# Moving the value splits and half of two normalisations between an attention loop and its output projection

## The chip, the cores and the metric

The kernel runs on one core of one Trainium2 chip. The metric is the device time of one execution in microseconds (us). The engines are TensorE (PE in the profile, its weight loads PEld), VectorE (DVE), ScalarE (ACT), GpSimd (POOL) and SyncE (SP), which issues most DMAs here.

## What is computed

The reference is a trunk of two layers over 1024 tokens of width 1024, in float32. In each layer three groups of attention heads work side by side on one input projection: A (4 heads, a 2-D neighbourhood), B (6 heads, a sliding window with a sink) and C (6 heads, dense). Each group's output is normalised over its own width, the three are joined, and one output projection follows. A gated feed-forward part closes the layer.

```python
ya = neighborhood_attention(...)          # width 256
yb = sliding_window_attention(...)        # width 384
yc = axial_attention(...)                 # width 384
ga, gb, gc = split_cols(g_group[l], GROUP_WIDTHS)
y = jnp.concatenate([rms_norm(ya, ga), rms_norm(yb, gb), rms_norm(yc, gc)], axis=-1)
x = x + gt_a * (y @ w_o[l])
```

## The kernel before

The kernel is written with a framework that traces the program, then orders each engine's instructions by its own estimate of their times. An instruction may be drawn ahead of others that stand before it in the text, unless it is pinned: `pin(engines, True)` makes each instruction of these engines follow the one that was pinned before it. All instructions pass through one helper, so the profile shows them under line 49.

Accuracy comes from splitting: a float32 operand is written as a high part `hi` in a matmul type and a low part `lo` with the rest, and a product takes three matmuls (`mm3`). ScalarE makes `hi`, VectorE makes `lo` from it.

The attention is a loop of steps n from -4 to 66 over a stream of 64 pairs (a pair is one head with 256 queries): pairs 0 to 23 are the C heads, 24 to 39 the A heads, 40 to 63 the B heads; A and B are the "band" heads. In a band step n:

- pair n + 4 is scored (TensorE, `sA` or `sB`, and VectorE adds the bias and takes the row's extreme value), pair n + 3 goes through the exponential (ScalarE), pair n + 2 is divided by its sums (a reciprocal on VectorE, `pr<-pr,rs` on GpSimd);
- pair n is transposed (`T<-identr,pr`) and split (`pt`: ScalarE the high part, VectorE the low part, the latter in step n + 1);
- pair n - 2 is multiplied with the values (`pv`); after every second pair ScalarE copies half of the result (`cmb`), in an odd step, and VectorE combines it into `y` at the start of the next step (`y<-pv,cmb`). One PSUM buffer holds `pv`, so the next pair's product waits for the combine.

In these steps TensorE, ScalarE, VectorE and GpSimd are pinned. After each step's body the list `later` runs what was noted for it, and a few things at fixed steps, unpinned but for GpSimd.

`y` holds the joined output as 8 chunks of 128 channels by 1024 tokens: chunks 0 and 1 are A, 2 to 4 B, 5 to 7 C. The output projection takes the chunks in the order `korder = (5, 6, 7, 0, 1, 2, 3, 4)` and works first on the first 512 tokens ("half 0"), then on the second ("half 1").

When a group's heads are done, its squares are summed in `gss` (tiles `gsq` on the way). `stats` then sums over channels with 16 one-column matmuls (`ps_st`) and takes the reciprocal root by Newton steps on VectorE (`isq`, `rstd`). `norm_scale` turns the roots into a row for each half (`spread`: four transposes into `ps_r`; ScalarE copies it to `rb`, of which there are two buffers shared with `gsq`) and returns one multiply per chunk and half (`y<-y,rb`). For C the statistics come at step 29, both spreads at step 32 and the six multiplies at steps 33 to 38; for A they come at 47, 50 and 51 to 54; all ten multiplies are on GpSimd. B's follow in the output projection, half on VectorE and half on GpSimd.

`y_split(k, half, hi, lo)` scales a chunk by its gain and splits it: one ScalarE and one VectorE instruction. For half 0 of chunks 5, 6, 7, 0, 1 the result lies in `yq` (`qk<-y` in the profile). Two of these five calls stand at steps 55 and 59, three in the output projection after its first weight block (`ki == 0`). Half 0 of the B chunks goes to `yb`, half 1 of all chunks to `y1` later (`y<-y,vecs` in the profile).

In the tail of the loop (from step 60) matmuls of the output projection for the first two chunks (`o_rows(0, ...)`, `o_rows(1, ...)`, into `ps_o`) stand between the last pairs, and weights of the projection are split (`whi`, `wlo`).

Of the kernel before, what the change touches and what calls it, by code (L numbers as in the profile page):

```python
# [85 lines left out]
def trunk(ctx: ExitStack, tc, A, C, out):  # L86
# [320 lines left out]
    def rstd_cols(ssqs, width, nt, sp_, psp, tag="mm", newton=False):  # L407

        ps = psp.tile([P, 512], F32, name="ps_st", tag=tag)
        for j in range(nt):  # L410
            for i, s in enumerate(ssqs):
                pe.matmul(
                    ps[:, j : j + 1],
                    s[:, j * P : (j + 1) * P],
                    ones,
                    start=(i == 0),
                    stop=(i == len(ssqs) - 1),
                )
        r = sp_.tile([P, 8], F32, name="rstd", tag="rstd", bufs=2)
        if newton:  # L420
            inv_sqrt(r[:, :nt], ps[:, :nt], width, sp_)
            return r
        act.activation(r[:, :nt], ps[:, :nt], AF.Sqrt, bias=epst, scale=1.0 / width)
        dve.reciprocal(r[:, :nt], r[:, :nt])
        return r
# [441 lines left out]
    for l in range(2):  # L867
# [770 lines left out]
            square(sq)  # L1638
            pool.tensor_tensor(out=ss[:, c], in0=ss[:, c], in1=sq, op=ALU.add)

        def norm_scale(chunks, r, psp, tag, engines):

            todo = []
            for half, eng in enumerate(engines):
                c = slice(half * H, (half + 1) * H)
                ps = spread(r, 4 * half, psp, tag=tag)
                rb = atp.tile([P, H], F32, name="rb", tag="rb", bufs=2)
                act.copy(rb, ps)
                for n in chunks:
                    todo.append(  # L1650
                        lambda eng=eng, n=n, c=c, rb=rb: eng.tensor_tensor(
                            out=y[:, n, c], in0=y[:, n, c], in1=rb, op=ALU.mult
                        )
                    )
            return todo
# [58 lines left out]
            23: ((5, 6, 7), 384.0), 39: ((0, 1), 256.0), 63: ((2, 3, 4), 384.0),  # L1714
        }
        begins = {23: 0, 39: 24, 63: 40}
        later = {}
        N = len(stream)
        pairs = {}
# [4 lines left out]
        for n in range(-AHEAD - 1, N + 3):  # L1724
            ahead = AHEAD if n + AHEAD < NC else AHEAD_B
            begin = range(done, min(n + ahead + 1, N))
            if n < 0:
                begin = range(done, done)
            elif n == 0:
                opened(*(pairs[i] for i in range(4)))  # L1730
                begin = range(3, 4)
                fresh = []
            elif n < NC:
                for i in range(2 if n > 1 else 0):
                    if 0 <= n:
                        pairs[n].turn(i)
                    while unfinished:
                        unfinished.pop(0)()
                    if 2 <= n - 1:
                        pairs[n - 1].pv(i)  # L1740
                    for m in begin:
                        if m < min(made, NC):
                            pairs[m].qk(i)
                for i in range(2 if n == 1 else 0):
                    pairs[begin[0]].qk(i)
                fresh = [pairs[m] for m in begin if NC <= m < made]
                for b in fresh:
                    b.scores()
                    b.exps()
                    b.divide()  # L1750
            else:
                for b in worked:
                    b.divide()
                if NC <= n - 1 < N:
                    pairs[n - 1].low()
                if NC <= n - 3:
                    pairs[n - 3].combine()
                fresh = [pairs[m] for m in begin if m < made]
                for b in fresh:
                    b.scores()  # L1760
                for b in scored:
                    b.exps()
                if n < N:
                    pairs[n].turn()
                if NC <= n - 2 < N:
                    pairs[n - 2].pv()
                    pairs[n - 2].fold()
                elif n == NC:
                    for i in range(2):
                        pairs[n - 1].pv(i)  # L1770
                scored, worked = fresh, scored
            done = max(done, min(begin.stop, made)) if n >= 0 else done
            while made < min(N, n + ahead + 2):
                for key, make in preload.get(made, []):
                    heads[key] = make()
                pairs[made] = stream[made][0]()
                made += 1
            if n >= 0:
                pin((pe, act, dve), False)
            for what in later.pop(n, []):  # L1780
                what()
            if n in (0, 6):
                for j in range(8):
                    (v_back if n else v_store)(j)
            if n == 4 and l == 0:
                rows_A(1)
                rows_B()
            if n == 6:
                pin((sp,), False)
            if n == 50:  # L1790
                yq = qk_tile()
            if n == 54:
                wst = [w_o_stage(k) for k in korder[:2]]
            if n in (55, 59):
                ki = (n - 55) // 4
                y_split(korder[ki], 0, yq[:, ki, 0:H], yq[:, ki, H:S])
            if n in (59, 61):
                w01.append(split_tile(wst.pop(0), 1, (atp, "pr", 6), dve))
            if n == 60:
                t2 = [psS.tile([P, 2, H], F32, name="ps_o", tag="S") for _ in range(2)]  # L1800
                pss = [t2[i // 2][:, i % 2, :] for i in range(NS)]
            if n in (61, 62):
                o_rows(0, w01[0], range(NS)[2 * (n - 61) : 2 * (n - 60)])
            if n in (63, 64):
                o_rows(1, w01[1], range(NS)[2 * (n - 63) : 2 * (n - 62)])
            if n == 62:
                wq = [w_rows(w_o, k * P, eng=dve) for k in korder[2:4]]
            m = n - 1 if n <= NC else n - 3
            for end, (chunks, width) in norms.items():
                if begins[end] <= m <= end and (m - begins[end]) % 8 == 7 and (n <= NC or m >= NC):  # L1810
                    i = (m - begins[end]) // 8
                    if end not in gss:
                        gss[end] = gss_tile()
                    for half in range(2):
                        what = lambda a=(chunks, gss[end], i, half, m == N - 1): norm_sum(*a)
                        if m == N - 1:
                            what()
                        else:
                            later.setdefault(n + 1 + half, []).append(what)
                    if m == end and end < N - 1:  # L1820

                        def stats(end=end, width=width, n=n, chunks=chunks):
                            r = rstd_cols([gss[end]], width, 8, atp, psT, tag="T", newton=True)

                            def scale():
                                todo = norm_scale(chunks, r, psT, "T", (pool, pool))
                                for i, what in enumerate(todo):
                                    later.setdefault(n + 9 + i, []).append(what)

                            later.setdefault(n + 8, []).append(scale)  # L1830

                        later.setdefault(n + 5, []).append(stats)
            pin((pe, act, dve), n < 0 or n >= NC - 1)
# [33 lines left out]
        for ki in range(5):  # L1867
            if ki < 2:
                o_rows(ki, w01[ki], range(NS, NK))
                w_ahead(3)  # L1870
            else:
                o_rows(ki, w_next(), range(NK))
            if ki == 0:
                for i in range(2, 5):
                    y_split(korder[i], 0, yq[:, i, 0:H], yq[:, i, H:S])
            if ki == 2:
                r = rstd_cols([gss[N - 1]], norms[N - 1][1], 8, atp, psl, newton=True)
            if ki == 3:
                for what in norm_scale(norms[N - 1][0], r, psl, "mm", (dve, pool)):
                    what()  # L1880
                yb = [
                    atp.tile([P, 3, H], F32R, name="yb", tag="zA", bufs=2) for _ in range(2)
                ]
                for i in range(3):
                    y_split(2 + i, 0, yb[0][:, i, :], yb[1][:, i, :])
# [661 lines left out]
```

## Time and profile before

| | us |
|---|---|
| median of 3 runs | 2385.76 (2385.19 to 2387.93) |
| profiled execution, device time | 2386.03 |
| its span, first to last instruction | 2384.3 |
| mean granted TensorE clock | 0.997 |
| TensorE / VectorE / ScalarE / GpSimd busy | 2330.1 / 1757.3 / 1186.5 / 781.9 |
| band steps of layer 0 and 1, from the first score of an A head to that of the last pair | about 380 to 466 and 1540 to 1626 |

Rows of a timeline give the start in us from the span's start, the duration, the engine, the line, the operation and `output<-inputs`, and in brackets the idle time of the engine before it and what ended it. Rows of groups give a count, the busy time, the mean duration in ns, and the idle time before. The clock is granted in full in all stretches that the prediction uses.

### The profile page before, as it was taken

The page shows a single profiled execution, that of the slowest core. Times are in us where ns is not written, and L with a number is a line of the kernel's source. Part 1 is how long each engine was busy: PE and PEld are TensorE (multiplying, and loading weights), DVE is VectorE, ACT ScalarE, POOL GpSimd, SP SyncE. Part 2 cuts the span into 40 slices and gives each one's busy share as a digit, 9 for nine tenths or more (in the row PEclk, how much of TensorE's full clock was granted, in tenths as well). Part 3 has the DMA queues.
Part 4 walks back from the last instruction along what each step waited for, and adds up shares of the span by engine and source line. Part 5 has one row for each costly group of instructions (what it writes and reads, how often), then busy time and mean ns, then how long its engine had stood idle before and what let it go on. Part 6 is the DMA issues. An engine that isn't in the chain of part 4 may idle for free. (4 is left out here: it accounts for less than half of the span.)

```text
span 2384.3 us, 33350 instructions
## 1 busy us (share of the span) xinstructions
PE 2330.1 (98%) x11733; PEld 1949.5 (82%) x11733; DVE 1757.3 (74%) x2754; ACT 1186.5 (50%) x2264; POOL 781.9 (33%) x747
## 2 busy tenths in 40 slices
PE   8999999999999999999999999999999999999998
PEld 5788898888788888788888889988888888888886
DVE  5777898967957687586777689987796664537765
ACT  4422788944543333344533158897454333334443
POOL 1441356810244444200135124575015443430001
PEclk9999999999999999999999999999999999999999
DMA  8567417164345444586434861242633443329743
GB/s 279 150 194 227 138 28 198 34 210 126 111 143 175 131 154 153 183 259 186 155 96 132 256 186 28 72 120 74 225 102 126 153 155 103 104 98 297 214 121 111
DMA packets 307416, 358.00 MB, mean 150 GB/s; under 512 B 51996, under 2 KB 223868, under 8 KB 307248
## 3 DMA queue, kind: packets, MB, share of 16 engines
q1 hardware_dynamic: 290752, 346.26, 46.6%
q10 hardware_dynamic: 16128, 9.44, 1.5%
q8 instruction: 92, 1.51, 0.3%
q14 instruction: 76, 0.62, 0.1%
q0 software_dynamic: 368, 0.17, 0.0%
HBM read 270.84 MB, written 88.63 MB: 151 GB/s over the span
## 5 line engine op out<-in xcount | busy, mean ns | idle before, releaser
L49 PE MATMUL ps_d<-wpt 128*128 128x512 f32 x1848 | 423.8, 390 | 1.0 <-ACT wpt L49 0.7
L49 PEld LDWEIGHTS ps_d<-wpt 128*128 128x128 f32 x1848 | 345.7, 188 | 74.4 <-issue 3.0
L49 POOL TENSOR_SCALAR pr<-pr,rs 128x1024 f32<-128x1024 f32 (+2 forms) x248 | 190.2, 781 | 188.7 <-DVE rs L49 171.1
L49 POOL TENSOR_TENSOR sg<-sg,u 128x512 f32<-128x512 f32 x82 | 126.8, 1548 | 347.1 <-ACT sg L49 221.6
L49 PE MATMUL pv<-pt,vs 128*128 128x256 f32 x1088 | 176.1, 296 | 16.3 <-DVE y L49 13.7
L49 ACT CAST wpt<-w 128x512 fp32r<-128x512 f32 x154 | 95.7, 621 | 175.7 <-PE ps_d L49 155.0
L49 DVE TENSOR_TENSOR pt<-T,pt 128x512 fp32r<-128x512 f32 x272 | 177.6, 680 | 7.0 <-ACT pt L49 5.9
L49 ACT CAST pt<-T 128x512 fp32r<-128x512 f32 x272 | 151.7, 586 | 42.4 <-PE T L49 40.7
L49 ACT COPY u<-ps_w 128x512 f32<-128x512 f32 x128 | 75.1, 586 | 192.0 <-PE ps_w L49 187.1
L49 DVE SCALAR_TENSOR_TENSOR acc<-wmt,condT,acc 128x512 f32<-128x512 f32 (+1 forms) x98 | 117.0, 1202 | 71.5 <-DMA wmt<-in_w_mod_dram 70.7
L49 DVE TENSOR_TENSOR wpt<-w,wpt 128x512 fp32r<-128x512 f32 x154 | 109.1, 708 | 79.7 <-ACT wpt L49 75.4
L49 POOL TENSOR_TENSOR wpt<-ws,wpt 128x512 fp32r<-128x512 f32 x80 | 110.7, 1384 | 171.2 <-ACT wpt L49 132.4
L49 PEld LDWEIGHTS pv<-pt,vs 128*128 128x128 f32 x1088 | 142.2, 189 | 29.7 <-DVE y L49 25.4
L49 PE MATMUL T<-identr,pr 128*128 128x128 f32 x1176 | 160.8, 273 | 0.8 <-ACT edge L49 0.4
L49 PEld LDWEIGHTS T<-identr,pr 128*128 128x128 f32 x1176 | 137.8, 140 | 15.5 <-ACT edge L49 1.1
L49 ACT CAST wpt<-ws 128x512 fp32r<-128x512 f32 x176 | 107.8, 622 | 51.4 <-issue 22.9
L49 DVE TENSOR_TENSOR wpt<-graw,wpt 128x512 fp32r<-128x512 f32 x154 | 110.2, 716 | 17.3 <-ACT wpt L49 17.3
L49 ACT CAST wpt<-graw 128x512 fp32r<-128x512 f32 x154 | 95.0, 617 | 51.7 <-DMA graw<-gpd 43.3
L49 DVE TENSOR_REDUCE rs<-sC 128x1 f32<-128x1024 f32 x88 | 107.2, 1220 | 12.5 <-PE sC L49 11.4
L49 DVE TENSOR_TENSOR wlo<-wst,whi 128x1024 fp32r<-128x1024 f32 (+1 forms) x70 | 91.6, 1313 | 33.3 <-ACT whi L49 29.4
L49 DVE TENSOR_TENSOR wpt<-ws,wpt 128x512 fp32r<-128x512 f32 x96 | 81.0, 852 | 47.5 <-ACT wpt L49 47.2
L49 DVE TENSOR_TENSOR ws<-wr 128x512 f32<-128x512 f32 x88 | 81.3, 924 | 46.5 <-POOL wpt L49 43.0
(308 smaller groups left out, 5966.1 us busy)
## 6 DMA issues: line engine op xcount, KB each, us to landing
wr<-in_w_gu_dram SPq DMA_DIRECT2D x92, 512.0 KB, 4.1
gpd<-sg SPq DMA_DIRECT2D x154, 256.0 KB, 4.4
graw<-gpd SPq DMA_DIRECT2D x76, 512.0 KB, 3.8
w<-in_w_down_dram SPq DMA_DIRECT2D x110, 256.0 KB, 5.0
wmt<-in_w_mod_dram SPq DMA_DIRECT2D x48, 512.0 KB, 5.7
qk<-qkd SPq DMA_DIRECT2D x44, 512.0 KB, 7.0
wst<-in_w_o_dram SPq DMA_DIRECT2D x32, 512.0 KB, 4.2
wmt<-in_w_mod_dram SPq DMA_DIRECT2D x64, 256.0 KB, 3.9
```

Source lines behind the costliest of these rows:

```text
L49: ins = op(*args, **kwargs)
```

## The change

Three things are changed, in both layers.

- The five value splits of half 0 are placed after steps 57, 61, 64, 65 and 66, all inside the loop, and pinned on ScalarE and VectorE.
- For C and A, only half 0 is normalised inside the loop: the spread (now pinned on TensorE and ScalarE) stands at step 32 for C as before and at step 60 for A instead of 50, and its three or two multiplies follow on GpSimd in the next steps.
- Half 1 of C and A is normalised in the output projection after the first weight block, by five multiplies on VectorE. Their reciprocal roots are held until then, in a third `rstd` buffer.

```diff
-        r = sp_.tile([P, 8], F32, name="rstd", tag="rstd", bufs=2)
+        r = sp_.tile([P, 8], F32, name="rstd", tag="rstd", bufs=3 if newton else 2)
...
-        def norm_scale(chunks, r, psp, tag, engines):
+        def norm_scale(chunks, r, psp, tag, halves):
...
-            for half, eng in enumerate(engines):
+            for half, eng in halves:
...
+        scales = {23: 32, 39: 60}
+        Y_SPLITS = (57, 61, 64, 65, 66)
+        held = []
...
-            if n in (55, 59):
-                ki = (n - 55) // 4
+            if n in Y_SPLITS:
+                ki = Y_SPLITS.index(n)
+                pin((act, dve), True)
                 y_split(korder[ki], 0, yq[:, ki, 0:H], yq[:, ki, H:S])
+                pin((act, dve), False)
...
+                            held.append((chunks, r))
+
                             def scale():
-                                todo = norm_scale(chunks, r, psT, "T", (pool, pool))
+                                pin((pe, act), True)
+                                todo = norm_scale(chunks, r, psT, "T", ((0, pool),))
+                                pin((pe, act), False)
                                 for i, what in enumerate(todo):
-                                    later.setdefault(n + 9 + i, []).append(what)
-
-                            later.setdefault(n + 8, []).append(scale)
+                                    later.setdefault(scales[end] + 1 + i, []).append(what)
+
+                            later.setdefault(scales[end], []).append(scale)
...
             if ki == 0:
-                for i in range(2, 5):
-                    y_split(korder[i], 0, yq[:, i, 0:H], yq[:, i, H:S])
+                for chunks, r in held:
+                    for what in norm_scale(chunks, r, psl, "mm", ((1, dve),)):
+                        what()
...
-                for what in norm_scale(norms[N - 1][0], r, psl, "mm", (dve, pool)):
+                for what in norm_scale(norms[N - 1][0], r, psl, "mm", ((0, dve), (1, pool))):
```

## The prediction, made before the result was known

> **What bounds the kernel now.** I read the profile from the outside in: the page's busy times, then the busy time of each engine by stretch, then who TensorE waited for, then the timelines of single engines around the places that the diff names. "Step n" below is one pass of the attention loop (n as in the code), which scores pair n + 4, transposes pair n and multiplies pair n - 2 with the values.
>
> ```profile
> PE 2330.1 (98%) x11733; PEld 1949.5 (82%) x11733; DVE 1757.3 (74%) x2754; ACT 1186.5 (50%) x2264; POOL 781.9 (33%) x747
> ```
>
> TensorE is busy for 2330.1 of the 2384.3 us span. Nothing in this edit removes a matmul, so all it can win are waits of TensorE, 54 us in the whole program. The next view gives busy times in stretches that I cut at the starts of score matmuls: steps 32 to 36, 37 to 45 (the first eight steps of band heads with no normalising in them), 47 to 59 (where the edit takes work out), then the tail of the loop and the start of the output projection; the last row is steps 47 to 59 of layer 1.
>
> ```profile
> core 0: us, PE busy (x) PEld busy (x) DVE busy (x) ACT busy (x) POOL busy (x), PEclk, DMA share, GB/s
> 398.22:408.26 10.04, 9.63 (x77) 8.97 (x76) 8.57 (x32) 9.46 (x28) 7.29 (x12) 1.00 0.91 261
> 410.94:429.47 18.53, 17.57 (x136) 16.39 (x134) 16.96 (x53) 17.76 (x54) 16.53 (x30) 1.00 0.52 160
> 433.94:466.44 32.50, 28.67 (x226) 27.10 (x224) 30.56 (x95) 30.97 (x87) 24.77 (x45) 1.00 0.05 14
> 466.44:492.69 26.25, 25.30 (x149) 21.11 (x148) 16.58 (x25) 16.01 (x33) 12.29 (x12) 1.00 0.40 121
> 492.69:524.58 31.89, 31.89 (x153) 26.56 (x152) 25.83 (x39) 15.66 (x22) 4.74 (x3) 1.00 0.57 203
> 1593.32:1625.84 32.52, 28.70 (x226) 27.12 (x224) 30.58 (x95) 30.96 (x87) 24.82 (x45) 1.00 0.05 14
> ```
>
> Three readings. In the quiet band steps (second row) ScalarE is busy for 17.76 of 18.53, TensorE for 17.57, VectorE for 16.96: three engines in step, none with room. In steps 47 to 59 TensorE falls to 28.67 of 32.50. In the output projection (fifth row) TensorE never stops, 31.89 of 31.89, while ScalarE is half idle. The waits of TensorE in the third row, then in the second:
>
> ```profile
> PE pv L49 <- DVE y L49: 3.8, 5, 1.3
> ```
>
> ```profile
> PE pv L49 <- DVE y L49: 0.8, 2, 0.4
> ```
>
> The product with the values waits for VectorE's combine (`y<-pv,cmb`), because one PSUM buffer holds it. It is 3.8 us in five waits against 0.8 in two: whatever stands before the combine on VectorE is paid for by TensorE.
>
> **What the edit takes away.** Quiet steps cost 18.53 / 8 = 2.316 us, so steps 47 to 59 would cost 12 x 2.316 = 27.80. The statistics of the A heads stand in them and stay:
>
> ```profile
> 436.07 1.84 PE L49 MATMUL ps_st<-onesr,gss 128*128 128x1 f32 x16
> 437.78 0.83 PE L49 MATMUL sB<-qk 128*128 128x256 f32 x4
> ```
>
> They hold TensorE for 437.78 - 436.07 = 1.71. What is left, 32.50 - 27.80 - 1.71 = 2.99 us, is the excess of layer 0; layer 1 gives 32.52, so 3.01. These rows (groups between 400 and 470 us) name its makers:
>
> ```profile
> L49 DVE SCALAR_TENSOR_TENSOR qk<-y,vecs,qk 128x512 fp32r<-128x512 f32 x5 | 4.8, 952 | 0.1
> ...
> L49 ACT ACTIVATE qk<-y,vecs 128x512 fp32r<-128x512 f32 x5 | 3.6, 724 | 0.0
> ...
> L49 ACT COPY rb<-ps_r 128x512 f32<-128x512 f32 x4 | 2.1, 581 | 0.0
> ```
>
> All five value splits (`qk<-y`, the tile `yq`) already run here, though three are written in the output projection: they are not pinned, and the scheduler drew them forward. They bring 3.6 us of ScalarE and 4.8 of VectorE into engines without room, and the A heads' spread adds two `rb` copies and eight transposes:
>
> ```profile
> 445.81 1.05 PE L49 MATMUL ps_r<-identr,rstd 128*128 128x128 f32 x8
> 446.61 0.66 PE L49 MATMUL sB<-qk 128*128 128x384 f32 x3
> ```
>
> 446.61 - 445.81 = 0.80 us of TensorE. The new places (57, 61, 64 to 66) leave one split in this stretch, and step 60 takes the spread out of it. So 2.99 us per layer are open to be won, 0.80 of them only moved. The ten GpSimd multiplies that become five win nothing by themselves: the last of the C heads' six still ran in the quiet stretch, where GpSimd was busy for 16.53 of 18.53 and the steps kept their pace.
>
> ```profile
> 417.31 1.28 POOL L49 TENSOR_TENSOR y<-y,rb 128x512 f32<-128x512 f32 x1
> ```
>
> **What it puts in their place.** First the split at step 57, now pinned behind that step's work on ScalarE and VectorE. Step 41 is the same kind of step (second pair of a head), quiet, so I lay the split into its rows:
>
> ```profile
> 422.40 0.67 DVE L49 TENSOR_TENSOR pt<-T,pt 128x512 fp32r<-128x512 f32 x1
> 423.26 0.69 DVE L49 TENSOR_TENSOR y<-pv,cmb 64x512 f32<-64x512 f32 x1 [0.19 <-ACT cmb L49]
> ```
>
> ```profile
> 422.65 0.58 ACT L49 COPY cmb<-pv 64x512 f32<-64x512 f32 x1
> ```
>
> ```profile
> 424.01 0.74 PE L49 MATMUL pv<-pt,vs 128*128 128x256 f32 x4
> ```
>
> ScalarE's half of the split follows the `cmb` copy (ends 423.23) and takes 0.72, to 423.96. VectorE's half is queued ahead of the next step's reciprocal, `pt` subtraction and combine, and waits for it: 0.74 (the `yb` rows below have the same shape), to 424.72. Then come about 0.1 of reciprocal, 0.6 and 0.69 for the other two, so the combine ends near 426.1 and the product with the values, which started at 424.01, starts 2.1 us later. I book 1.8, since the quiet steps have a wait of up to 0.4 soon after that a late product absorbs. Floating, the five splits and their company cost 2.99 - 0.80 = 2.2 together, some 0.4 each; both ends, 0.4 and 2.1, stay for the range, and I am near the upper one because the order is written out.
>
> Second, the C heads' spread at step 32, now half of it and pinned:
>
> ```profile
> 401.29 1.04 PE L49 MATMUL ps_r<-identr,rstd 128*128 128x128 f32 x8
> 402.08 0.59 PE L49 MATMUL sA<-qk 128*128 128x384 f32 x2
> ```
>
> Steps 32 to 36 took 10.04 against 4 x 2.316 = 9.26, so 0.78, which is the 0.79 of these transposes; the two copies cost nothing. Half of them would save 0.39; but the pinned copy now waits on ScalarE for transposes that stand behind the step's product, so I take 0.2, with 0 and 0.39 as ends. Third, four transposes move to step 60, 0.40, and eight to the output projection, 0.80, both at full price: in the fourth row TensorE is busy for 25.30 of 26.25 and in the fifth all the time. Fourth, in the tail the splits at 61 to 66 (0.72 and 0.74 each) stand before combines again, but output-projection matmuls lie ready to fill TensorE; I take 0.2 of wait, bounds 0 and 2.1.
>
> Fifth, the multiplies on VectorE after the first weight block. The last band heads' chain runs there:
>
> ```profile
> 488.30 0.69 DVE L49 TENSOR_TENSOR y<-pv,cmb 64x512 f32<-64x512 f32 x1
> 494.57 0.17 DVE L49 TENSOR_SCALAR isq<-ps_st 128x8 f32<-128x8 f32 x1 [5.57 <-PE ps_st L49]
> ```
>
> ```profile
> 489.80 1.29 POOL L49 TENSOR_TENSOR gss<-gss,gsq 128x512 f32<-128x512 f32 x1 [3.85 <-ACT gsq L49]
> ```
>
> ```profile
> 504.32 3.11 DVE L49 SCALAR_TENSOR_TENSOR yb<-y,vecs,yb 128x512 fp32r<-128x512 f32 x3
> ```
>
> ```profile
> 508.26 0.39 PE L49 MATMUL ps_o<-yb,whi 128*128 128x512 f32 x1
> ```
>
> VectorE stands idle for 5.57 us; five multiplies of 0.69 need 3.5. The first `yb` is ready near 504.32 + 3.11 / 3 = 505.4 and needed at 508.26, a slack of 2.9. The pinned split of step 65 delays the last combine by 0.72 + 0.74 = 1.5, and the A heads' copy needs the buffer that GpSimd's last addition frees at 491.1. That fits, so I book nothing. The cover is the 5.57; the price without it is the second rival. No moved step issues a DMA, so SP's queue stays as it is; on GpSimd the A heads' two multiplies now come behind the last scaling of probabilities, where nobody waits but the last `gss` additions; and the third `rstd` buffer only lets two reciprocal roots live on until the projection.
>
> ```profile
> L49 DVE TENSOR_TENSOR y<-y,rb x3: 694/1784/1801, 500.3 to 502.6; 128x512 f32<-128x512 f32 x3
> L49 POOL TENSOR_TENSOR y<-y,rb x3: 1323/1740/1742, 500.8 to 503.8; 128x512 f32<-128x512 f32 x3
> L49 ACT ACTIVATE yb<-y,vecs x3: 724/725/725, 501.0 to 504.4; 128x512 fp32r<-128x512 f32 x3
> L49 DVE SCALAR_TENSOR_TENSOR yb<-y,vecs,yb x3: 739/739/1781, 504.3 to 506.7; 128x512 fp32r<-128x512 f32 x3
> ```
>
> The same multiply takes 0.69 alone and 1.78 beside GpSimd's, from these rows. The Trainium skill (SBUF — State Buffer, Who interferes with whom) gives the cause: a VectorE instruction with two SBUF inputs and a GpSimd instruction that reads SBUF exclude each other for their whole length. By that rule only the multiplies that meet GpSimd's last addition would be slow; the trace agrees, as only instructions beside a GpSimd one show 1.78.
>
> The sum per layer: 2.99 won; 1.8 + 0.40 + 0.80 + 0.2 lost; 0.2 won at step 32: 0.0 us. Twice that leaves the profiled execution at its 2386.03 us (span 2384.3 and 1.73 around it), which lies 0.27 over the median of 2385.76; on the median it is 2385.8.
>
> **The rivals.** *Faster*: the pinned order hides the splits. For it speaks step 32, where two copies vanished in the pace. Then all 2.99 go, 0.39 at step 32, and also the 26.25 - 25.30 = 0.95 of waits in the tail, less 1.20 of moved transposes: 3.13 per layer, 6.3 in all, 2379.5. Against it speaks that the combine directly follows the split in the queue.
>
> *Slower*: the `yb` chain loses its cover. If the multiplies get their `rb` only after GpSimd's last addition, they stand before the reciprocal root on VectorE: 1.5 late, three multiplies at 0.69 and two beside GpSimd at 1.78 make 1.5 + 2.1 + 3.6 = 7.2, less the slack of 2.9 is 4.3 per layer, 8.6 in all, 2394.4. It decides when the first `isq` starts later than 494.57 + 2.9 relative to the first `yb` matmul. Against it: two buffers exist, and the C heads' copy needs only the earlier one.
>
> *Nothing moves*: the scheduler places multiplies and copies where the old ones had room, and the pinned splits come out as costly as the floating ones: 2385.8 too.
>
> **The numbers.** About 0.2% (4.8 us) is what a measurement of this kernel can tell from no change. Forecast 2385.8: 0.48; nothing moves: 0.06; faster rival: 0.24; slower rival: 0.22. The forecast's own unknowns (1.8 between 0.4 and 2.1, 0.2 between 0 and 2.1 in the tail, 0.2 between 0 and 0.39) make -1.8 to +2.4 per layer, so 2382.2 to 2390.6. The range takes in most of the faster rival and the nearer part of the slower one: 2380 to 2392. Faster by over 0.2%: 0.24; within: 0.54; slower: 0.22.
>
> **What would show it.** Right: steps 49 to 57 of band heads at 2.3 us each, `qk<-y` at five fixed places, one wait of about 2 us for `y` at step 58, no wait for `yb`. Wrong towards faster: no such wait. Wrong towards slower: TensorE idle before the first `yb` matmul, or more than 0.95 us idle in the tail.

## Result and profile after

The changed kernel takes 2394.09 us (median of 8 runs, 2391.21 to 2395.68) where the kernel before takes 2385.62 beside it (2384.62 to 2387.93): ratio 1.0032, 95% interval 1.0022 to 1.0042. It is slower by about 8 us. The forecast of 2385.8 is wrong, and the time lies above the range. The profiled execution of the changed kernel took 2391.75 us (span 2390.0).

TensorE's busy time at the head of the page hardly says why, since matmuls at a lower granted clock count as busy for longer:

```profile
PE 2333.4 (98%) x11733; PEld 1951.9 (82%) x11733; DVE 1765.9 (74%) x2764; ACT 1188.5 (50%) x2264; POOL 768.9 (32%) x737
```

So I cut both traces at the same instructions: the start of step 47, the last band-head score, and the first `yb` matmul. First the kernel before, from the last score to the `yb` matmuls (layers 0 and 1); the stretches ahead of these stand in the prediction. Columns: start and end, length, busy time by engine, granted clock, DMA share, GB/s.

```profile
466.44:508.26 41.82, 40.87 (x228) 34.16 (x227) 28.58 (x45) 24.43 (x44) 17.03 (x15) 1.00 0.33 101
1625.84:1667.55 41.71, 40.89 (x229) 34.17 (x228) 28.65 (x45) 24.48 (x44) 17.04 (x15) 1.00 0.33 101
```

The changed kernel, steps 47 to 59 and the tail of each layer:

```profile
433.75:464.97 31.22, 27.76 (x217) 26.29 (x216) 27.09 (x91) 28.96 (x83) 17.57 (x41) 1.00 0.05 14
464.97:510.84 45.87, 43.67 (x240) 36.67 (x239) 36.08 (x57) 29.20 (x51) 21.14 (x17) 0.96 0.30 94
1595.08:1626.28 31.20, 27.75 (x217) 26.27 (x216) 27.09 (x91) 28.97 (x83) 17.56 (x41) 1.00 0.06 14
1626.28:1672.93 46.65, 43.71 (x240) 36.92 (x239) 36.37 (x57) 29.31 (x51) 20.13 (x17) 0.96 0.29 91
```

The band steps gain 32.50 - 31.22 = 1.28 us. The tail loses 45.87 - 41.82 = 4.05 in layer 0 and 4.94 in layer 1, where 1.4 was booked. Two things in these rows go beyond the sum: TensorE idles for 2.20 and 2.94 us in the tail instead of 0.95 and 0.82 (length less busy), where the sum had 0.2 more, and the granted clock is 0.96, for which it had nothing. Slices of 5 us around the two places, the kernel before and then the changed one:

```profile
480.00:485.00 5.00, 4.87 (x26) 3.88 (x25) 3.12 (x4) 2.92 (x6) 0.34 (x1) 1.00 0.58 187
1625.00:1630.00 5.00, 4.52 (x31) 3.89 (x32) 4.97 (x14) 4.97 (x13) 3.50 (x5) 1.00 0.00 0
```

```profile
480.00:485.00 5.00, 3.31 (x18) 2.84 (x18) 3.89 (x6) 3.27 (x5) 1.27 (x1) 0.84 0.56 183
485.00:490.00 5.00, 5.00 (x20) 4.02 (x19) 4.00 (x5) 3.22 (x5) 0.66 (x1) 0.82 0.62 177
1625.00:1630.00 5.00, 4.41 (x25) 4.44 (x26) 4.86 (x13) 3.22 (x8) 3.58 (x6) 0.69 0.00 0
1630.00:1635.00 5.00, 5.00 (x35) 4.59 (x35) 2.25 (x7) 4.17 (x10) 4.92 (x6) 0.97 0.32 105
```

(0.16 + 0.18) x 5 = 1.70 us in layer 0 and (0.31 + 0.03) x 5 = 1.70 in layer 1: the same amount in both, 3.4 us at half speed, each time behind waits of TensorE. These are the waits (idle time in brackets):

```profile
464.28 0.71 PE L49 MATMUL pv<-pt,vs 128*128 128x256 f32 x4 [2.38 <-DVE y L49]
468.80 0.50 PE L49 MATMUL ps_o<-qk,wlo 128*128 128x512 f32 x1 [0.51 <-DVE wlo L49]
481.28 0.50 PE L49 MATMUL ps_o<-qk,whi 128*128 128x512 f32 x1 [1.24 <-ACT qk L49]
482.46 0.74 PE L49 MATMUL pv<-pt,vs 128*128 128x256 f32 x4 [0.45 <-DVE y L49]
```

```profile
1625.59 0.71 PE L49 MATMUL pv<-pt,vs 128*128 128x256 f32 x4 [2.39 <-DVE y L49]
1638.51 0.74 PE L49 MATMUL ps_o<-qk,whi 128*128 128x512 f32 x2 [0.69 <-DVE qk L49]
1644.02 0.50 PE L49 MATMUL ps_o<-qk,whi 128*128 128x512 f32 x1 [0.98 <-ACT qk L49]
1649.94 0.50 PE L49 MATMUL ps_o<-qk,whi 128*128 128x512 f32 x1 [1.27 <-ACT qk L49]
```

The first wait of each layer is the forecast one at step 58. The 0.45 us in front of `pv` has its like in the kernel before (0.47 us at 477.25); the waits for `qk` are new. Such a wait is for a split that came too late for the projection. ScalarE's rows just before the one of 1.24 us:

```profile
479.90 0.58 ACT L49 COPY cmb<-pv 64x512 f32<-64x512 f32 x1
480.51 0.72 ACT L49 ACTIVATE qk<-y,vecs 128x512 fp32r<-128x512 f32 x1
```

The split of step 64 is pinned behind the copy of `pv` of step 63. TensorE, through with the 24 projection matmuls that the loop has for the first two chunks, needs the third and waits for it.

The loss of each layer is counted from the first statistics matmul of the C heads to the first `y` matmul of the second half. The kernel before, then the changed one, layers 0 and 1:

```profile
392.39:524.58 132.19, 125.59 (x825) 112.04 (x824) 109.32 (x279) 101.27 (x251) 74.88 (x115) 1.00 0.42 133
1551.77:1683.87 132.10, 125.63 (x826) 112.08 (x825) 109.01 (x278) 100.85 (x250) 74.97 (x115) 1.00 0.40 124
```

```profile
392.08:527.64 135.56, 127.66 (x825) 113.37 (x824) 111.84 (x285) 101.96 (x251) 68.08 (x110) 0.99 0.43 133
1553.38:1689.73 136.35, 127.69 (x825) 113.60 (x824) 112.15 (x285) 102.13 (x251) 67.06 (x110) 0.99 0.40 124
```

Layer 0 loses 3.37 us: 1.70 of clock, 1.30 of idle time (7.90 less 6.60) and 0.48 of slower `yb` matmuls, which add up to 0.1 more than the loss. Layer 1 loses 4.25: 1.70, 2.19 and 0.48, again 0.1 more. Together that is 7.6 us. The profiled span grew by only 5.7, since the rest of it came out 1.9 shorter, 1.45 of it between the two stretches (1027.19 us before, 1025.74 after). The edit changes nothing there, and over all the traces of this case that part varies between 1025.7 and 1028.0 us. The median grew by 8.5.

### The profile page after: what moved, and what is told of

It is laid out like the page before. It is cut to its first block, busy times and chain, and to the rows that moved or that the text cites. A ratio compares the mean times of both kernels' runs of the same rounds, so it can differ in the third digit from the quotient of the medians.

```text
span 2390.0 us, 33362 instructions
## 1 busy us (share of the span) xinstructions
PE 2333.4 (98%) x11733; PEld 1951.9 (82%) x11733; DVE 1765.9 (74%) x2764; ACT 1188.5 (50%) x2264; POOL 768.9 (32%) x737
```

## The experiments

Three causes were named before the first runs: PLACES, the pinned splits; NORMS, the normalising moved to the projection; and SHIFT, an address. The third `rstd` buffer, 32 bytes a partition, moves what follows it in its pool by as much, and the `yb` matmuls grew by 7 ns each. Groups of the `yb` matmuls, before and after:

```profile
L49 PE MATMUL ps_o<-yb,whi 128*128 128x512 f32 x48 | 14.9, 389 | 0.0
```

```profile
L49 PE MATMUL ps_o<-yb,whi 128*128 128x512 f32 x48 | 15.3, 396 | 0.0
```

All results in one table. "Layer" is the stretch of 132.19 and 132.10 us above; "idle" is TensorE's, 90 us less its busy time in 440 to 530 and 1600 to 1690 us (behind step 32, so without the waits there); "drops" counts the 1.7 us low-clock events in these two windows. Medians are beside the kernel before on the same chip. The last three columns are from one execution of each kernel, the profiled one. In e5_even and e6_first56 it was the slowest of 11 (2390.36 and 2392.64 us), so their drops are those of one execution, not of the median.

| kernel | median, before | ratio (95%) | layer 0 / 1 | idle 0 / 1 | drops 0 / 1 |
|---|---|---|---|---|---|
| before | | 1 | 132.19 / 132.10 | 4.79 / 4.64 | 0 / 0 |
| changed | 2394.09, 2385.62 | 1.0032 (1.0022 to 1.0042) | 135.56 / 136.35 | 5.66 / 6.39 | 1 / 1 |
| a1_shift32 | 2388.0, 2386.81 | 1.0003 (0.9994 to 1.0012) | 132.83 / 132.98 | 4.62 / 4.74 | 0 / 0 |
| e1_splits | 2392.32, 2386.81 | 1.0022 (1.0013 to 1.0031) | 135.28 / 134.90 | 5.72 / 5.53 | 1 / 1 |
| e2_norms | 2389.58, 2386.81 | 1.0011 (1.0002 to 1.0020) | 133.42 / 133.45 | 4.95 / 4.97 | 0 / 0 |
| e3_pad64 | 2393.76, 2386.81 | 1.0029 (1.0019 to 1.0040) | 135.45 / 134.77 | 5.55 / 6.18 | 1 / 0 |
| e4_unpinned | 2388.13, 2386.36 | 1.0009 (1.0000 to 1.0017) | 133.29 / 133.38 | 4.94 / 4.85 | 0 / 0 |
| e5_even | 2388.84, 2386.36 | 1.0010 (1.0001 to 1.0019) | 133.20 / 133.84 | 4.40 / 4.78 | 0 / 0 |
| e6_first56 | 2389.86, 2386.36 | 1.0017 (1.0008 to 1.0026) | 134.17 / 136.44 | 4.16 / 5.22 | 1 / 2 |
| e8_splits_even | 2388.33, 2386.36 | 1.0009 (1.0000 to 1.0018) | 132.71 / 132.84 | 5.08 / 5.13 | 0 / 0 |
| w1_warm | 2391.59, 2386.57 | 1.0023 (1.0015 to 1.0032) | 135.08 / 134.48 | 4.46 / 4.99 | 1 / 0 |
| w2_three | 2388.67, 2386.57 | 1.0011 (1.0002 to 1.0020) | 132.29 / 132.44 | 4.73 / 4.95 | 0 / 0 |
| w3_both | 2387.99, 2386.57 | 1.0006 (0.9997 to 1.0015) | 133.07 / 132.97 | 4.64 / 4.56 | 0 / 0 |
| n1_nosplits | 2382.57, 2385.84 | 0.9987 (0.9978 to 0.9996) | 130.06 / 130.73 | 2.66 / 2.75 | 0 / 0 |

**a1_shift32**: the kernel before with the third buffer alone.

```diff
-        r = sp_.tile([P, 8], F32, name="rstd", tag="rstd", bufs=2)
+        r = sp_.tile([P, 8], F32, name="rstd", tag="rstd", bufs=3 if newton else 2)
```

> The kernel before with the third rstd buffer alone: every engine's order is that of before, only the tiles of the attention pool lie 32 bytes elsewhere. Theory PLACES (the pinned splits stall TensorE at step 58 and between steps 62 and 66, and the clock drops behind the stalls) and theory NORMS (the second-half normalising delays the projection): same as before within 1.5 us, except that matmuls with yb may show 396 instead of 389 ns, 144 x 7 ns = 1.0 us. Theory SHIFT (the 32 bytes make most of the loss): slower by 5 us or more.

The `yb` matmuls take 396 ns, 0.48 us per layer; the time, 1.2 us above with an interval from -1.4 to +2.9, shows no more than that. SHIFT is real and small.

**e1_splits**: the kernel before with the splits alone.

```diff
+        Y_SPLITS = (57, 61, 64, 65, 66)
-            if n in (55, 59):
-                ki = (n - 55) // 4
+            if n in Y_SPLITS:
+                ki = Y_SPLITS.index(n)
+                pin((act, dve), True)
                 y_split(korder[ki], 0, yq[:, ki, 0:H], yq[:, ki, H:S])
+                pin((act, dve), False)
...
-                for i in range(2, 5):
-                    y_split(korder[i], 0, yq[:, i, 0:H], yq[:, i, H:S])
```

> The kernel before with the five splits pinned at steps 57, 61, 64, 65, 66, the normalising as before. PLACES: slower by 5 to 10 us, one wait of about 2.4 us for y at step 58 in each layer, waits for the split tile in the tail, stretches of granted clock under 1. NORMS: faster by up to 3 us, since the splits leave the full steps. SHIFT: faster by up to 3 us.

5.5 us slower, two thirds of the change's loss, with the 2.38 us wait at step 58 in the trace and a drop of the clock in each layer.

**e2_norms**: the changed kernel with the five split calls back as in the kernel before (the diff of e1_splits reversed), and four `rstd` buffers.

> The changed normalising alone (half 0 of the A heads at step 60, half 1 of C and A on VectorE in the projection), the splits where they stood before and unpinned; four rstd buffers, so the pool lies 64 bytes from before. PLACES: within 2 us of before, no wait over 1.4 us for y, the granted clock 1.00 in all stretches. NORMS: slower by 6 to 9 us, with TensorE idle ahead of the first yb matmul. SHIFT: within 2 us.

2.8 us slower, with no drop. The floating splits show where: chunks 0 and 1 (A) now cannot be split before GpSimd's multiplies behind step 60. They come in the tail. There ScalarE waits 1.50 us for GpSimd, and the weight cast and the `cmb` copy come behind that split; the combine needs the copy, and TensorE waits for the combine.

```profile
478.66 0.72 ACT L49 ACTIVATE qk<-y,vecs 128x512 fp32r<-128x512 f32 x1 [1.50 <-POOL y L49]
479.30 1.03 ACT L49 CAST whi<-wst 128x1024 fp32r<-128x1024 f32 x1
481.00 0.58 ACT L49 COPY cmb<-pv 64x512 f32<-64x512 f32 x1
```

```profile
483.56 0.74 PE L49 MATMUL pv<-pt,vs 128*128 128x256 f32 x4 [1.50 <-DVE y L49]
```

5.5 and 2.8 make 8.3, the change's 8.5 within the noise: the two halves of the edit add up.

**e3_pad64**: the changed kernel with four `rstd` buffers instead of three.

> The changed kernel with four rstd buffers instead of three, so that the attention pool is moved by 64 bytes instead of 32; everything else as changed. PLACES and NORMS: slower than before by 6 to 8 us (1 us less than the change for the yb matmuls at most). SHIFT: the loss is gone, within 1.5 us of before.

The `yb` matmuls take 394 ns; 2393.76 us. The address is not the cause of the loss.

**e4_unpinned**: the changed kernel without the two `pin` lines around `y_split`.

> The changed kernel with the five split calls at the same steps (57, 61, 64, 65, 66), only no longer pinned to their place in the written order, so that the scheduler may put each of them later, or where its engine has room. Three readings of what the splits cost. PIN (the fixed order is the cost): the wait of the product with the values at step 58 falls from 2.4 to under 0.6 us per layer, and about 5 us of the 8 come back: 2388 to 2390, what is left being the normalising in the projection. FIRST (the place of the first split, an odd step whose split stands ahead of the next combine) and LATE (three splits at 64 to 66 stand ahead of the last combines, TensorE runs out of products and its granted clock falls behind that): the call stands where it stood, so the time stays at 2392 to 2395 with some 4 us or more lost per layer in the tail.

All but 1.8 of the change's 8.5 us come back. The scheduler drew three of the splits forward to 440 to 446 us and put the two others at 476 and 478, where they stand in e2_norms as well, and the layers are as long as there (133.3 and 133.4 us). The step-58 wait is gone:

```profile
463.65 0.74 PE L49 MATMUL pv<-pt,vs 128*128 128x256 f32 x4 [0.27 <-DVE y L49]
```

The fixed order at these places costs, as PIN said. The expectation set FIRST and LATE against it, wrongly: without the pin no split stays at its step, so this run cannot tell the three apart, and the next two had to.

**e6_first56** and **e5_even**: the changed kernel with other places.

```diff
-        Y_SPLITS = (57, 61, 64, 65, 66)
+        Y_SPLITS = (56, 61, 64, 65, 66)     # e6_first56
+        Y_SPLITS = (56, 58, 60, 62, 64)     # e5_even
```

> The changed kernel with only the first split moved, from step 57 to step 56; the four others stay at 61, 64, 65, 66. FIRST: the wait of 2.4 us for y at step 58 goes, two layers make 4.8 us less, 2389 to 2390. LATE: the idle time at 468 to 485 us and the low granted clock stay, and the step-58 wait either stays or turns up again in the tail: 2392.5 to 2394. Were both true, 2389 to 2391 with the clock still under 0.9 in the slices at 480 to 490 us.

> The changed kernel with the five pinned splits at steps 56, 58, 60, 62, 64 instead of 57, 61, 64, 65, 66: each behind an even step, one every second step, none behind the last two steps of the loop. The normalising stays as changed. FIRST and LATE together (places): no wait for y over 1 us from step 56 on, granted clock 1.00 throughout, and the tail loses only the 1.2 us of moved transposes and 0.5 of yb matmuls per layer: 2385 to 2388. PIN: three splits stand in steps 56 to 60, where the band heads have no room, each costs about 2 us as the one at 57 did: 2394 to 2398. NORMS (the normalising in the projection is the main cost): 2390 or more.

Moving one split by one step, from behind an odd step to behind an even one, takes the 2.4 us wait down to 1.07, and 5 us off the loss (3.5 above the kernel before, not 8.5): FIRST holds. But with the late places kept, the clock in the profiled execution still drops, once in layer 0 and for twice as long in layer 1, where TensorE waited 2.64 us for a late split:

```profile
1643.22 0.80 PE L49 MATMUL ps_o<-qk,whi 128*128 128x512 f32 x1 [2.64 <-ACT qk L49]
```

```profile
1640.00:1645.00 5.00, 2.36 (x7) 1.25 (x6) 3.73 (x5) 3.55 (x6) 0.00 (x0) 0.76 0.47 161
1645.00:1650.00 5.00, 5.00 (x20) 4.53 (x20) 2.96 (x4) 3.87 (x6) 1.27 (x1) 0.56 0.30 89
```

With even, early places (e5_even) its trace has no drop and no wait for a late split; the same slice:

```profile
1640.00:1645.00 5.00, 4.79 (x25) 3.75 (x24) 4.94 (x7) 3.54 (x7) 0.00 (x0) 1.00 0.44 128
```

So LATE holds in the traces; the times, 2389.86 and 2388.84, differ by less than their intervals tell apart. PIN as a rule (each pinned split costs 2 us wherever it stands, 2394 or more) falls with e5_even. Its 2388.84 is still 0.8 above what places alone were to give.

**e8_splits_even**: the kernel before with the diff of e1_splits, at steps 56, 58, 60, 62, 64.

> The kernel before with its normalising untouched, only the five splits pinned at steps 56, 58, 60, 62, 64. Places: the band stretch to the last band-head score, 74.1 us per layer in the kernel before, comes down to 72 to 73 (the floating splits' 2.2 us go in part), the tail keeps its 41.8 and the last weight rows their 16.3: 2382 to 2385, a little faster than the kernel before. PIN: each fixed split holds back a combine, as at step 57, 2390 or more. Nothing moves (the scheduler's own places were as good): 2385 to 2387.

The expectation of a gain failed. The band steps did fall, as hoped, and the tail gave it back (steps 47 to 59 and tail, layer 0):

```profile
433.70:464.79 31.09, 28.95 (x225) 27.18 (x224) 27.12 (x91) 29.05 (x84) 22.54 (x45) 1.00 0.05 14
464.79:508.58 43.79, 40.85 (x229) 34.23 (x228) 32.65 (x52) 28.25 (x49) 19.18 (x15) 1.00 0.32 98
```

The idle time is 5.1 us per layer where it was 4.7: it moved.

**w1_warm**: e1_splits with more work for TensorE in the wait of step 58.

```diff
-                    pairs[n].turn()
+                    pairs[n].turn(4 if n == 58 else 1)   # its four transposes four times over
```

> The kernel with the pinned splits alone (57, 61, 64, 65, 66; normalising as before), in which step 58 issues its four transposes of probabilities four times over into the same tile: 12 more transposes, some 1.2 us of TensorE work (0.10 each in the rows of five or six), all of it inside the 2.38 us in which TensorE stood idle in front of the product with the values. Nothing is saved by it; it only shortens the idle stretch to about 1.2 us. CLOCK (the 1.7 us lost behind that stall in each layer is the granted clock, which falls because TensorE stood idle): no slice from 460 to 475 us and from 1620 to 1640 us under 0.95, and the time falls by 2 x 1.7 us in spite of the added work, from 2392.3 to about 2389. NOT CLOCK (the drop has another cause, or the rows behind the stall are slow for something else): 2392 to 2395.

At that place no slice falls under 1.00 in either layer, as CLOCK said. First the slice behind the wait in layer 0 of e1_splits; then, of w1_warm, the rows that fill the wait, the same slice, and a later one:

```profile
465.00:470.00 5.00, 4.78 (x27) 4.81 (x28) 4.24 (x12) 2.96 (x8) 3.54 (x5) 0.66 0.02 3
```

```profile
462.11 2.12 PE L49 MATMUL T<-identr,pr 128*128 128x128 f32 x18
465.30 0.71 PE L49 MATMUL pv<-pt,vs 128*128 128x256 f32 x4 [1.07 <-DVE y L49]
```

```profile
465.00:470.00 5.00, 4.18 (x31) 3.78 (x32) 4.97 (x14) 4.55 (x12) 3.58 (x6) 1.00 0.00 2
480.00:485.00 5.00, 3.44 (x18) 2.54 (x17) 3.87 (x5) 3.50 (x7) 0.91 (x1) 0.87 0.63 202
```

By itself this could be chance: the same wait of 2.4 us has no drop behind it in layer 0 of the changed kernel and in neither layer of e3_pad64. The traces say more when they are cut on a grid. In each trace every stretch of low clock starts a whole number of times 3.41 us after the first one (which is at 33 to 36 us). Windows of this grid, two pairs of the changed kernel and then three windows around the step-58 wait of e3_pad64:

```profile
479.99:483.40 3.41, 1.72 (x11) 1.24 (x11) 3.14 (x5) 2.08 (x4) 0.18 (x1) 1.00 0.75 248
483.40:486.81 3.41, 3.41 (x14) 3.02 (x13) 2.45 (x2) 2.95 (x4) 1.09 (x1) 0.50 0.08 23
1623.46:1626.87 3.41, 1.28 (x10) 1.31 (x11) 3.35 (x10) 3.37 (x10) 1.23 (x4) 1.00 0.00 0
1626.87:1630.28 3.41, 3.41 (x19) 3.41 (x18) 3.31 (x8) 1.60 (x6) 3.33 (x4) 0.50 0.00 0
```

```profile
459.72:463.13 3.41, 2.52 (x21) 2.25 (x19) 1.81 (x7) 3.10 (x9) 0.30 (x2) 1.00 0.00 0
463.13:466.54 3.41, 1.91 (x16) 1.95 (x17) 3.35 (x10) 3.37 (x9) 1.86 (x5) 1.00 0.02 5
466.54:469.96 3.42, 2.91 (x21) 2.34 (x20) 3.42 (x8) 2.99 (x10) 3.34 (x3) 1.00 0.00 0
```

TensorE idles for 1.69 and 2.13 us of the first window of a pair, and the clock is at half for the whole next one. In e3_pad64 the edge of a window cuts the wait, 0.89 and 1.50 us, and no drop follows. Over all the traces, each of the eight times that the clock falls in the stretches of the table follows a window with 1.56 to 2.38 us of idle time, and no window under 1.5 us is followed by one; the largest without, in layer 1 of e3_pad64, has between 1.6 and 1.7. So what counts is the idle time within one window, and the limit lies near half of it. In w1_warm the filled wait leaves at most 1.07 us in any window there: CLOCK holds.

The time missed the expected 2389: 2391.59. In layer 0 a drop came 18 us later instead, behind the late splits (last row of the slices), where waits of 1.11 and 0.45 us fall in one window. Filling one wait does not help where the next ones add up to as much.

**w2_three** and **w3_both**: places 56, 60, 62, and the last two splits pinned behind the first weight block of the projection; w2 on the kernel before, w3 on the changed one with the filler ahead of the band bias tiles cut.

```diff
+        Y_SPLITS = (56, 60, 62)
...
             if ki == 0:
+                pin((act, dve), True)
+                for i in range(3, 5):
+                    y_split(korder[i], 0, yq[:, i, 0:H], yq[:, i, H:S])
+                pin((act, dve), False)
...
-        pad(atp, 16)          # w3_both only
+        pad(atp, 8)
```

> The kernel before with its normalising untouched and the splits at the places that the runs so far favour: pinned at steps 56, 60 and 62, the last two pinned behind the first weight block of the output projection, where VectorE stands idle for 5.6 us. CONSERVED (the idle time of TensorE only moves: ScalarE and VectorE have to do the five splits before TensorE can go on, wherever they stand): TensorE idles 5.4 to 6.2 us per layer from the first band score to the yb matmuls, as in the kernel before (5.8) and with five pinned at even steps (6.2), and the time is 2385 to 2388. PLACES (a place exists that hides them): idle time under 4.5 us per layer, 2382 to 2384.

> The changed kernel's normalising with the same places (56, 60, 62, two in the projection), and the filler in front of the band bias tiles cut from 16 to 8 words a partition, so that the third rstd buffer no longer moves what follows it. SHIFT: the yb matmuls take 389 ns again instead of 396, 0.48 us per layer. CONSERVED: idle time 5.4 to 6.2 us per layer, 2386 to 2388. PLACES: 2382 to 2384. If the normalising in the projection costs something of its own, this kernel is 1 us or more above the other kernel with these places.

Neither beats the kernel before. The `yb` matmuls of w3_both take 389 ns again, which confirms SHIFT as an address effect. The idle time is 4.6 to 4.95 us, much the same as before, so CONSERVED describes what was tried. (The 5.4 to 6.2 of the expectations were read from the waits in brackets from about step 36 on, a longer stretch; read so, w2_three has 5.9 and 6.1 and w3_both 5.6.) With w3_both at 1.0006 (0.9997 to 1.0015), the changed normalising costs nothing that the time can show once the splits stand well and the address is put right; in the traces the layers of w3_both are 0.78 and 0.53 us longer than those of w2_three.

**n1_nosplits**: the kernel before without the five splits.

```diff
-                hi, lo = yq[:, ki, 0:H], yq[:, ki, H:S]
+                q = pairs[N - 1].q
+                hi, lo = q[:, 0:H], q[:, H:S]
...
-                y_split(korder[ki], 0, yq[:, ki, 0:H], yq[:, ki, H:S])
-                    y_split(korder[i], 0, yq[:, i, 0:H], yq[:, i, H:S])
```

> The kernel before with the five value splits of the first half left out altogether: the output projection multiplies the weights with the last band head's queries instead, which lie there in the same type, so that every matmul is issued and the numbers are not the projection's. It gives the most that any place of these five splits can win. FLOOR as the prediction's sum had it: 2.99 - 0.80 = 2.2 us per layer are the price of the five splits in the band heads, so the idle time of TensorE from the first band score to the yb matmuls falls from 5.8 to about 3.6 per layer and the time by 4.4 us, to 2381 to 2383. CONSERVED (the splits only bring forward waits that the loop's own chain of ScalarE and VectorE has anyway): the idle time stays above 5 us and the time falls by less than 2 us, 2384.5 to 2386.5.

2382.57, 3.3 us below the kernel before: FLOOR, within its 2381 to 2383. The window of 90 us in layer 0, before and without splits:

```profile
440.00:530.00 90.00, 85.21 (x494) 73.25 (x493) 72.70 (x148) 60.89 (x129) 38.35 (x51) 1.00 0.38 127
```

```profile
440.00:530.00 90.00, 87.34 (x503) 75.08 (x502) 70.38 (x146) 58.84 (x125) 36.18 (x51) 1.00 0.40 134
```

87.34 - 85.21 = 2.1 us of TensorE time is what the five splits cost in layer 0 where the scheduler had put them, and 1.9 in layer 1; the layers get shorter by 2.13 and 1.37. So some 3.5 us in all is the most that any place could have won, and none of the places tried won any of it.

## Why the prediction was wrong

**Right.** The excess of steps 47 to 59 and its makers: n1_nosplits puts the five splits at 2.1 and 1.9 us of idle time, the prediction had 2.2. The wait at step 58: its mechanism and place (ScalarE's half waited for the `cmb` copy, as laid out), and its size nearly (2.38 us, booked 1.8, upper end 2.1). Together the band steps were to gain 2.99 - 1.8 = 1.2 and gained 1.28. The twelve moved transposes: TensorE's extra time in the tail of layer 0, 4.05, is 1.20 of transposes, 1.25 of idle time and 1.70 of clock, which sum to 4.15.

**The step that failed** is the fourth of "What it puts in their place": 0.2 us of wait in the tail, because "output-projection matmuls lie ready to fill TensorE". They do not lie ready: they need the very splits that were pinned late. The prediction looked at what a split delays on VectorE, not at who reads the split. The tail idles 1.25 and 2.12 us more than before, where 0.2 was booked; its own upper bound, 2.1, is about what came.

**What was missing** is the granted clock. Every stretch that the prediction read shows it at 1.00, and no term allowed for its fall: 1.7 us per layer, as much as the forecast stall. The Trainium skill (TensorE: Matmul & The Clock Gate, What's actually happening) says that the clock falls to half after an idle window of about 3.4 us, and that the window runs free. The trace agrees on the amount (3.4 us at half speed is 1.7) and on the window that runs free (the grid under w1_warm), which brings in chance: e3_pad64 idles for 5.55 and 6.18 us, and drops only in the layer that idles less. It differs on the condition: no window had to be idle throughout, 1.56 of 3.41 us sufficed, and no wait in front of a drop was longer than 2.7 us.

**Small misses.** Step 32 was to win 0.2, and its steps take 0.20 more (16.07 us from the statistics on, 15.87 before): the pinned `rb` copy waits on ScalarE, the doubt that the prediction names, but beyond its lower end of 0, since the next product then waits too.

```profile
401.56 0.59 ACT L49 COPY rb<-ps_r 128x512 f32<-128x512 f32 x1 [0.90 <-PE ps_r L49]
405.38 0.74 PE L49 MATMUL pv<-pt,vs 128*128 128x256 f32 x4 [0.43 <-DVE y L49]
```

The third `rstd` buffer was said "only" to keep two roots alive; it cost 0.48 per layer, the slower `yb` matmuls.

**The rivals.** The time came out at the *slower* rival's 2394.4, but not by its mechanism. The five multiplies found their cover, and TensorE did not wait for `yb`:

```profile
492.14 3.10 DVE L49 TENSOR_TENSOR y<-y,rb 128x512 f32<-128x512 f32 x5 [2.83 <-ACT rb L49]
496.36 0.17 DVE L49 TENSOR_SCALAR isq<-ps_st 128x8 f32<-128x8 f32 x1 [1.12 <-PE ps_st L49]
```

```profile
510.84 0.40 PE L49 MATMUL ps_o<-yb,whi 128*128 128x512 f32 x1
```

The multiplies end 1.1 us ahead of the reciprocal root (`isq`), and the first `yb` matmul has no idle time in brackets. What decided was the other sign that the prediction gives towards slower, more than 0.95 us idle in the tail. *Faster* fell with the step-58 wait. The scheduler's freedom with the splits, which the change took away, was worth 6.7 us (e4_unpinned).

**Open.** Where exactly the limit of idle time in a window lies is not settled: both outcomes occur between 1.5 and 1.7 us. In e2_norms and e4_unpinned the sums close within 0.2 us once the idle time is taken over the whole layer stretch (0.6 to 0.8 us more than before, and 0.48 of `yb`). In e5_even and w3_both 0.5 to 0.7 us per layer is neither idle time, clock nor address, and I could not assign it.

## What to carry to other kernels

Before an operation is moved, ask both who waits behind it on its engine and who reads its result; "there is work to fill the gap" holds only if that work does not need the thing moved. Where TensorE is 98% busy, price an added wait at more than its length: waits that fill about half of one 3.4 us window cost 1.7 us of granted clock on top. And measure the floor (the work left out) before looking for better places: here it was about 2 us per layer, and no fixed order that was tried beat the kernel's floating one.

## What was unexpected of the hardware

- The clock falls for whole windows of 3.41 us on a grid that runs through the execution, 1.7 us lost for each. Behind windows in which TensorE idled for 1.56 us or more it mostly fell, with no wait longer than 2.7 us; the same 2.4 us wait cost a drop or none, by where the edge of a window cut it.
- The record of a matmul of 128x512 with `yb` lasts 389 ns, 396 when the third buffer moves the pool by 32 bytes a partition, and 394 by 64 bytes. The 72 of them, which overlap, take 16.32 us in the first case and 16.80 in both others.
